# A values product of attention that is half native fp32 and half split operands

## The chip, the cores and the metric

The kernel runs on one core of a Trainium2 chip. The metric is the device time of one execution in microseconds (us): 1172.9 us before the change, the median of three runs that lie between 1172.45 and 1174.26 us.

## What is computed

The reference is a two-layer backbone over 512 latent tokens and 256 context tokens of width 1024. Layer 0 mixes tokens by pooling, layer 1 by attention, and each is followed by a squared-ReLU MLP with a hidden width of 4096. All inputs and the output are fp32. The change lies in the attention of layer 1, where 512 latent queries look at all 768 keys (6 tiles of 128), with 8 query heads of width 128 on 2 key/value heads:

```python
def attend(q, k, v):
    s = jnp.einsum('bqhgd,bkhd->bhgqk', q, k).astype(jnp.float32) * (HEAD_DIM ** -0.5)
    p = jax.nn.softmax(s, axis=-1).astype(v.dtype)
    return jnp.einsum('bhgqk,bkhd->bqhgd', p, v)
```

## The kernel before

**Split operands.** Almost every product is made of three TensorE matmuls: an fp32 operand is kept as a high half (`hi`, the value rounded to the reduced fp32 type `F32R`) and a low half (`lo`, the remainder), and hi·hi, hi·lo and lo·hi are added in PSUM. Each split costs one copy on ScalarE (ACT), which writes `hi`, and one subtraction on VectorE (DVE), which writes `lo`. A few products are native: both operands are plain fp32 and there is one matmul in the program.

**Order of the work.** The author places each helper at a time in a list (`Steps`), and the scheduler of the framework then sets the order on every engine from its own timing model. Each engine works its list in order, so an instruction that waits holds up all that stands behind it.

**Attention.** First the keys, values and queries are projected (`project`, L1064, tile `psq`); `kv_e` (L1120) splits the values of key tile t into `vH`, `vL` in the large buffer `rb`, and `kv_b`/`kv_c` normalise and transpose the keys. Then come 32 steps, `steps[i] = (h, t)`: head h (8) by block t of 128 queries (4). A step goes through these stages, each named by the line at which the profile shows it:

- `q_head` (once for a head): four transposes L1225 (tile `pq`), copy L1226 on ACT, subtraction L1227 on DVE.
- `s_scores`: six matmuls L1237 of 384 columns (tile `pss`, two PSUM tiles in turn), the row maximum L1241 on DVE, and the exponential L1242 on ACT, which also sums the row. It writes the row of 768 probabilities to one of four buffers, `pbuf(i % 4)`.
- `s_norm`: the reciprocal L1248 on DVE, and the scaling of the row, which a table of 32 truth values gives to DVE (L1250, 17 steps) or to ACT (L1252, 15 steps).
- `s_turn`: six transposes L1262 (tile `pspt`, one PSUM bank of the four of `psB` for each three key tiles), and for each three a copy L1264 on ACT and a subtraction L1265 on DVE, into `pTH` and `pTL`.
- `s_values` (after every second step, for 256 queries): 18 matmuls L1276 (tile `po`), three for each of the 6 key tiles, then copy L1278 on ACT and subtraction L1279 on DVE into `oH`, `oL`.

Between them stand the splits of the weights `w_o`, which follow attention: four loads of 1 MB into the three `raw` buffers, each split in quarters (L142 on ACT, L145 on DVE). Two of them are split during attention and two at its end, when `unit[1]` and `unit[2]` are free. These two units are one tile, `units`, opened once at the end of the first stage; during attention they hold `pTH`, `pTL` and the queries of the later heads. After attention comes the product with `w_o` (L1302, tile `psy`).

Of the kernel before, what the change touches and what calls it, by code (L numbers as in the profile page):

```python
# [17 lines left out]
P = 128  # L18
# [24 lines left out]
class Steps:  # L43
# [3 lines left out]
    def at(self, t, fn, *args):  # L47
        self.items.append((t, len(self.items), fn, args))
# [20 lines left out]
def backbone(ctx: ExitStack, tc, x, ctx_in, w_ada, w_pool, pool_scale, w_qkv, g_q, g_k, w_o, w_mlp_in,  # L69
# [39 lines left out]
    unit, pinned = [rb[:, 6144:10240]], [True]  # L109

    def open_units():
        rawe.close()
        pools[0] = rawp
        units = ctx.enter_context(tc.tile_pool(name="units", bufs=1)).tile([P, 2 * 4096], F32R, name="units")
        unit.extend(units[:, 4096 * i: 4096 * (i + 1)] for i in range(2))
# [35 lines left out]
    class Ring:  # L151
# [1 line left out]
            self.slots, self.n, self.halves = slots, 0, halves  # L153

        def load(self, src, width, pin=False, wait=None):
            raw = raw_load(src, rawp)
# [639 lines left out]
    st.at(200, open_units)  # L796
    st.run()

    pso = {}
# [233 lines left out]
    vH = rb[:, 3072:4608].rearrange("p (t n) -> p t n", n=256)  # L1033
    vL = rb[:, 4608:6144].rearrange("p (t n) -> p t n", n=256)
# [156 lines left out]
    def before0():  # L1191
# [8 lines left out]
        for t in (4, 5, 0, 1, 2, 3):  # L1200
# [6 lines left out]
    qTs = [(z[:, 0:512], z[:, 512:1024]) for z in (unit[0][:, 0:1024], unit[0][:, 1024:2048],  # L1207
                                                    unit[1][:, 3072:4096], unit[2][:, 3072:4096])]
    qbuf = lambda h: qTs[h if h < 2 else 2 + h % 2]
    pTH = unit[2][:, 0:NT * LAT].rearrange("p (s n) -> p s n", n=LAT)  # L1210
    pTL = unit[1][:, 0:NT * LAT].rearrange("p (s n) -> p s n", n=LAT)
    pbuf = lambda i: (xr[:, 4, 0:TOK], xr[:, 5, 0:TOK], gate[:, 1, 0:TOK], acc[:, 4 * D:4 * D + TOK])[i]
    aring = Ring([ra[:, 8192:12288], unit[0], unit[1], unit[2]])

    def wo_unit(ch, kk, wait=None):
        return aring.load(w_o[ch, kk], 512, True, wait)
# [29 lines left out]
    def s_norm(i):  # L1246
        sm, p = smx[i], pbuf(i % 4)
        ve.reciprocal(sm[:, 2:3], sm[:, 1:2])  # L1248
        if (False,False,False,True,False,True,True,True,True,True,True,True,False,False,True,False,True,False,True,False,True,True,True,False,False,True,False,False,False,False,True,True)[i]:
            ve.tensor_scalar(out=p, in0=p, scalar1=sm[:, 2:3], scalar2=None, op0=ALU.mult)  # L1250
        else:
            sc.activation(p, p, AF.Copy, scale=sm[:, 2:3])  # L1252

    def s_turn(i):
        _, t = steps[i]
        sl = slice(t * P, (t + 1) * P)
        p = pbuf(i % 4)
        for b in range(2):
            ps = psB.tile([P, 3, P], F32, tag="b", name="pspt")
            for j in range(3):  # L1260
                k = 3 * b + j
                te.transpose(ps[:, j, :], p[:, k * P:(k + 1) * P], ident)  # L1262
            hi, lo = pTH[:, 3 * b:3 * b + 3, sl], pTL[:, 3 * b:3 * b + 3, sl]
            sc.copy(hi, ps)  # L1264
            ve.tensor_tensor(out=lo, in0=ps, in1=hi, op=ALU.subtract)  # L1265

    def s_values(i):
        h, t = steps[i]
        half = t // 2
        kv = h // 4  # L1270
        hs = slice(kv * HD, (kv + 1) * HD)
        qs = slice(256 * half, 256 * half + 256)
        po = psB.tile([P, 512], F32, tag="b", name="po")
        for kt in range(NT):
            for n, (v, p) in enumerate(((vH, pTH), (vL, pTH), (vH, pTL))):
                te.matmul(po[:, 0:256], v[:, kt, hs], p[:, kt, qs],  # L1276
                          start=(kt == 0 and n == 0), stop=(kt == NT - 1 and n == 2))
        sc.copy(oH[:, h, qs], po[:, 0:256])  # L1278
        ve.tensor_tensor(out=oL[:, h, qs], in0=po[:, 0:256], in1=oH[:, h, qs], op=ALU.subtract)  # L1279

# [36 lines left out]
    def attention(st, base, unit_t):  # L1317
        at = lambda i, fn, *args: st.at(base + unit_t * i, fn, *args)
        for i, (h, t) in enumerate(steps):
            if t == 0:  # L1320
                at([-2, 3, 4.542, 7.928, 13.236, 15.602, 19.752, 23.755][h], q_head, h)
            at(i + 0.2, s_scores, i)
            at(i + 1.3, s_norm, i)
            at(i + 3.1, s_turn, i)
            if t % 2:
                at(i + 5.2, s_values, i)
        raws = []
# [134 lines left out]
```

## Time and profile before

| | us |
|---|---|
| median of three runs | 1172.9 |
| the profiled execution, its whole time | 1173.48 |
| its span in the trace | 1171.7 |
| TensorE (PE) busy | 1143.0 (98%) |
| weight loads (PEld) busy | 989.2 (84%) |
| VectorE (DVE) busy | 938.4 (80%) |
| ScalarE (ACT) busy | 636.7 (54%) |
| start of the first score matmul, of the last values matmul | 673.7, 780.0 |

Times in the trace count from the start of the span. A matmul's row shows the time from its issue to the end of its drain; matmuls that follow each other overlap, so the pace of a run of n equal ones is (time of the run − time of one) / (n − 1). A number in square brackets at the end of a row is idle time of the engine ahead of it and what ended it.

### The profile page before, as it was taken

The page shows a single profiled execution, that of the slowest core. Times are in us where ns is not written, and L with a number is a line of the kernel's source. Part 1 is how long each engine was busy: PE and PEld are TensorE (multiplying, and loading weights), DVE is VectorE, ACT ScalarE, POOL GpSimd, SP SyncE. Part 2 cuts the span into 40 slices and gives each one's busy share as a digit, 9 for nine tenths or more (in the row PEclk, how much of TensorE's full clock was granted, in tenths as well). Part 3 has the DMA queues.
Part 4 walks back from the last instruction along what each step waited for, and adds up shares of the span by engine and source line. Part 5 has one row for each costly group of instructions (what it writes and reads, how often), then busy time and mean ns, then how long its engine had stood idle before and what let it go on. Part 6 is the DMA issues. An engine that isn't in the chain of part 4 may idle for free.

```text
span 1171.7 us, 15966 instructions
## 1 busy us (share of the span) xinstructions
PE 1143.0 (98%) x6172; PEld 989.2 (84%) x6172; DVE 938.4 (80%) x1538; ACT 636.7 (54%) x1082; POOL 67.0 (6%) x120
## 2 busy tenths in 40 slices
PE   7899999999999999999999999999899999999997
PEld 5579899889899988998887889988888888888886
DVE  4688687989988997996778599877787779778876
ACT  4577655555454534555675388852776436535522
POOL 2030000000000000000241200001100000000001
PEclk9899999999999999999999999999999999999999
DMA  9884213343334334343423101115234124314312
GB/s 375 354 318 154 72 45 135 133 159 109 144 144 144 144 137 147 112 144 108 180 73 107 37 1 37 37 73 197 91 138 150 61 84 144 108 36 144 108 37 107
DMA packets 25516, 147.32 MB, mean 126 GB/s; under 512 B 2785, under 2 KB 5217, under 8 KB 9698
## 3 DMA queue, kind: packets, MB, share of 16 engines
q1 hardware_dynamic: 25442, 146.32, 34.2%
q8 instruction: 48, 0.79, 0.3%
q14 instruction: 26, 0.21, 0.1%
HBM read 138.96 MB, written 7.34 MB: 125 GB/s over the span
## 4 chain that ended last, share of the span: by engine, by line
PE 49%; issue 42%; POOL 3%; DVE 2%; ACT 2%; DMA 1%; SPq 0%; POOLq 0%; DVEq 0%; ACTq 0%
PE pso L817 22%; PE psin L691 18%; PE psin L567 3%; PE psq L1064 2%; PE pspool L65 1%; POOL rs L185 1%; PE psada L65 1%; PE pspool L490 1%; POOL rs L1073 1%; DMA raw<-in_w_ada 1%; DMA xr<-in_x 1%; PE psada L227 1%; POOL ms L183 1%; DVE ra L65 0%; ACT junk L170 0%
## 5 line engine op out<-in xcount | busy, mean ns | idle before, releaser
L817 PE MATMUL pso<-units,rb 128*128 128x512 f32 x1152 | 278.2, 392 | 0.0
L817 PEld LDWEIGHTS pso<-units,rb 128*128 128x128 f32 x1152 | 214.8, 188 | 41.2
L273 DVE SCALAR_TENSOR_TENSOR rows<-raw,cond,rows 128x256 f32<-128x256 f32 x280 | 126.5, 475 | 2.0
L829 DVE TENSOR_TENSOR acc<-acc,pso 128x512 f32<-128x512 f32 x129 | 85.1, 674 | 41.4 <-PE pso L817 41.2
L567 PE MATMUL psin<-ra,rb 128*128 128x512 f32 (+1 forms) x432 | 103.3, 340 | 1.8 <-ACT ra L364 1.6
L921 PE MATMUL pso<-units,pairs 128*128 128x512 f32 x336 | 82.3, 389 | 0.0
L567 PE MATMUL psin<-ra 128*128 128x512 f32 x256 | 80.5, 390 | 0.0
L567 PEld LDWEIGHTS psin<-ra,rb 128*128 128x128 f32 x432 | 69.9, 189 | 11.3 <-ACT ra L364 1.9
L921 PEld LDWEIGHTS pso<-units,pairs 128*128 128x128 f32 x336 | 63.1, 188 | 13.1
L925 DVE TENSOR_TENSOR acc<-acc,pso 128x512 f32<-128x512 f32 x72 | 48.7, 681 | 28.8 <-PE pso L921 28.8
L183 POOL TENSOR_SCALAR ms<-ss 128x1 f32<-128x1 f32 x20 | 11.4, 572 | 998.3 <-ACT junk L170 946.1
L691 PE MATMUL psin<-ra,units 128*128 128x384 f32 x336 | 65.5, 337 | 0.4 <-ACT psin L703 0.4
L691 PE MATMUL psin<-sums,units 128*128 128x384 f32 x336 | 63.9, 337 | 0.0
L691 PEld LDWEIGHTS psin<-ra,units 128*128 128x128 f32 x336 | 59.7, 188 | 3.9 <-ACT psin L703 0.9
L691 PEld LDWEIGHTS psin<-sums,units 128*128 128x128 f32 x336 | 58.9, 188 | 1.7
L145 DVE TENSOR_TENSOR units<-raw,units 128x1024 fp32r<-128x1024 f32 (+2 forms) x49 | 55.1, 1148 | 4.5 <-ACT units L142 4.4
L567 PEld LDWEIGHTS psin<-ra 128*128 128x128 f32 x256 | 48.0, 188 | 10.0
L142 ACT CAST units<-raw 128x1024 fp32r<-128x1024 f32 (+2 forms) x49 | 46.8, 994 | 14.0 <-PE pso L817 10.2
L827 ACT COPY acc<-pso 128x512 f32<-128x512 f32 x48 | 27.2, 588 | 48.9 <-PE pso L817 48.6
L567 PE MATMUL psin<-rb 128*128 128x512 f32 (+1 forms) x144 | 52.6, 367 | 0.2 <-DVE rb L365 0.2
L1064 PE MATMUL psq<-units,ra 128*128 128x512 f32 x216 | 51.7, 392 | 0.0
L567 PE MATMUL psin<-rb,ra 128*128 128x512 f32 x128 | 49.8, 389 | 0.0
(279 smaller groups left out, 2346.7 us busy)
## 6 DMA issues: line engine op xcount, KB each, us to landing
raw<-in_w_ada SPq DMA_DIRECT2D x48, 1024.0 KB, 4.9
raw<-in_w_mlp_in SPq DMA_DIRECT2D x32, 1024.0 KB, 4.9
raw<-in_w_mlp_out SPq DMA_DIRECT2D x32, 1024.0 KB, 5.3
raw<-in_w_qkv SPq DMA_DIRECT2D x6, 1024.0 KB, 4.8
spill<-xr SPq DMA_DIRECT2D x10, 512.0 KB, 4.2
xr<-spill SPq DMA_DIRECT2D x10, 512.0 KB, 6.8
raw<-in_w_o SPq DMA_DIRECT2D x4, 1024.0 KB, 4.8
xr<-in_x SPq DMA_DIRECT2D x4, 512.0 KB, 5.2
```

The costliest lines, as they stand in the source:

```text
L65: return lambda *args, **kw: self.tc.keep_in_program_order(f(*args, **kw))
L142: a = sc.copy(hi, raw)
L145: b = ve.tensor_tensor(out=lo, in0=raw, in1=hi, op=ALU.subtract)
L273: ve.scalar_tensor_tensor(out=r, in0=raw[:, k, :], scalar=cond[:, k, c:c + 1], in1=r, op0=ALU.mult, op1=ALU.add)
L567: te.matmul(ps[:, bank, o:o + ln], w[:, k, fs], rhs, start=start, stop=(k == KT - 1 and n == 2), skip_group_check=len(ks) < KT)
L691: te.matmul(bank, w[k], a[k], start=start and k == 0 and m == 0, stop=stop and k == 3 and m == 2, skip_group_check=True)
L817: te.matmul(pss[h][:, 0:cols[h][1]], a[:, f, ts_], w[:, f, cols[h][0]:sum(cols[h])], start=(n == 0 and not seeded[t]), stop=(n == len(seq) ...
L827: sc.copy(d, ps)
L829: ve.tensor_tensor(out=d, in0=d, in1=ps[:, 0:w], op=ALU.add)
L921: te.matmul(ps, a, w, start=(m == 0), stop=(m == len(seq) - 1))
L925: ve.tensor_tensor(out=M[n][:, t], in0=M[n][:, t], in1=ps, op=ALU.add)
L1064: te.matmul(ps, a[:, k, sl], w[:, k % 4, :], start=(k == 0 and n == 0), stop=(k == KT - 1 and n == 2))
```

## The change

**Values product.** Key tiles 0 to 2 are multiplied in native fp32 (one matmul in place of three), tiles 3 to 5 in split operands as before: 3 + 9 matmuls in place of 18. So the values of tiles 0 to 2 are copied as fp32 into `xr` row 4 and have no `lo`, and the first three transposed tiles of a step are copied as fp32 into `pT` and have no subtraction.

**Scaling.** All 32 rows are scaled on DVE; the table is gone.

**Buffers.** Two probability buffers, `pT`, the two halves `pTh` and the queries of heads 2 to 7 (`qs`) lie in a pool `soft`, which is opened over the memory of `units` at step 1.1 and closed at step 37.5, when `units` is opened anew. The last two `w_o` loads are issued at the same places as before, but get their unit only then. Normalised keys move to `xr` row 5 and have two buffers in place of four. The first stage is unchanged (`end_loads`).

The core of the diff:

```diff
+    values = lambda: xr[:, 4, 0:768].rearrange("p (t n) -> p t n", n=256)
+    vH = rb[:, 3072:3840].rearrange("p (t n) -> p t n", n=256)
+    vL = rb[:, 3840:4608].rearrange("p (t n) -> p t n", n=256)
...
     def kv_e(t):
         ps = pj[t]
-        sc.copy(vH[:, t, :], ps[:, 256:512])
-        ve.tensor_tensor(out=vL[:, t, :], in0=ps[:, 256:512], in1=vH[:, t, :], op=ALU.subtract)
+        if t < 3:
+            sc.copy(values()[:, t, :], ps[:, 256:512])
+        else:
+            sc.copy(vH[:, t - 3, :], ps[:, 256:512])
+            ve.tensor_tensor(out=vL[:, t - 3, :], in0=ps[:, 256:512], in1=vH[:, t - 3, :], op=ALU.subtract)
...
-        kf = xr[:, 4, 256 * (t % 4):256 * (t % 4) + 256]
+        kf = xr[:, 5, 512 + 256 * (t % 2):768 + 256 * (t % 2)]
...
+    def open_soft():
+        uheld[0].close()
+        pool = uheld[0].enter_context(tc.tile_pool(name="soft", bufs=1))
+        qs = pool.tile([P, 2 * 1024], F32R, name="qs")
+        qTs.extend((qs[:, 1024 * i:1024 * i + 512], qs[:, 1024 * i + 512:1024 * i + 1024]) for i in range(2))
+        halves = pool.tile([P, 2, 3, LAT], F32R, name="pTh")
+        soft["t"] = pool.tile([P, 3, LAT], F32, name="pT"), halves[:, 0], halves[:, 1]
+        ps = [pool.tile([P, TOK], F32, name=f"p{i}") for i in range(2)]
+        soft["p"] = ps
+
+    def close_soft():
+        uheld[0].close()
+        open_units()
+        aring.slots[2:] = unit[1:]
...
-        if (False,False,False,True,False,True,True,True,True,True,True,True,False,False,True,False,True,False,True,False,True,True,True,False,False,True,False,False,False,False,True,True)[i]:
-            ve.tensor_scalar(out=p, in0=p, scalar1=sm[:, 2:3], scalar2=None, op0=ALU.mult)
-        else:
-            sc.activation(p, p, AF.Copy, scale=sm[:, 2:3])
+        ve.tensor_scalar(out=p, in0=p, scalar1=sm[:, 2:3], scalar2=None, op0=ALU.mult)
...
-            hi, lo = pTH[:, 3 * b:3 * b + 3, sl], pTL[:, 3 * b:3 * b + 3, sl]
-            sc.copy(hi, ps)
-            ve.tensor_tensor(out=lo, in0=ps, in1=hi, op=ALU.subtract)
+            full, hi, lo = (z[:, :, sl] for z in soft["t"])
+            if b == 0:
+                sc.copy(full, ps)
+            else:
+                sc.copy(hi, ps)
+                ve.tensor_tensor(out=lo, in0=ps, in1=hi, op=ALU.subtract)
...
-        for kt in range(NT):
-            for n, (v, p) in enumerate(((vH, pTH), (vL, pTH), (vH, pTL))):
-                te.matmul(po[:, 0:256], v[:, kt, hs], p[:, kt, qs],
-                          start=(kt == 0 and n == 0), stop=(kt == NT - 1 and n == 2))
+        full, hi, lo = soft["t"]
+        seq = [(values()[:, kt, hs], full[:, kt, qs]) for kt in range(3)]
+        seq += [(v[:, kt, hs], p[:, kt, qs]) for kt in range(3) for v, p in ((vH, hi), (vL, hi), (vH, lo))]
+        for n, (v, p) in enumerate(seq):
+            te.matmul(po[:, 0:256], v, p, start=(n == 0), stop=(n == len(seq) - 1))
...
+        at(1.1, open_soft)
+        at(37.5, close_soft)
...
         for kk in range(2):
-            at((23.386, 25.741)[kk], lambda kk: wo[1].append(wo_unit(1, kk, raws)), kk)
+            at((23.386, 25.741)[kk], lambda kk: late.append(raw_load(w_o[1, kk], rawp)), kk)
+            at(37.6, lambda kk: wo[1].append(aring.place(late[kk], 512, raws)), kk)
```

**What moves.** The scheduler orders anew what stands in attention. On TensorE, from the sixth values product on, the order was (scores `pss`, transposes `pspt`, values `po`):

```order
L1276 MATMUL po<-units,rb 128x256 x18
L1262 MATMUL pspt<-ident,gate 128x128 x3
L1237 MATMUL pss<-rb,units 128x384 x6
L1262 MATMUL pspt<-ident,gate 128x128 x3
L1262 MATMUL pspt<-ident,acc 128x128 x6
L1276 MATMUL po<-units,rb 128x256 x18
L1237 MATMUL pss<-rb,units 128x384 x6
```

and in the changed kernel, whose scores stand at L1261, transposes at L1283 and values at L1302 (`p_5952` and `p_5953` are the two new probability buffers):

```order
L1302 MATMUL po<-pT,xr 128x256 x3
L1302 MATMUL po<-pTh,rb 128x256 x9
L1261 MATMUL pss<-rb,qs 128x384 x6
L1283 MATMUL pspt<-ident,p_5953 128x128 x6
L1261 MATMUL pss<-rb,qs 128x384 x5
L1283 MATMUL pspt<-ident,acc 128x128 x3
L1261 MATMUL pss<-rb,qs 128x384
```

The scores and transposes keep their places between the values products; the product itself becomes three native matmuls and nine on halves.

On DVE, around the second quarter of the first `w_o` split (L145), the order before was (L1241 maximum, L1250 scaling, L1265 subtraction of a transposed half, L1279 subtraction of an output half):

```order
L145 TENSOR_TENSOR ra<-raw,ra 128x512
L1279 TENSOR_TENSOR ra<-po,ra 128x256
L1248 RECIPROCAL sm<-sm 128x1
L1241 TENSOR_REDUCE sm<-pss 128x1
L1250 TENSOR_SCALAR gate<-gate,sm 128x768
L1265 TENSOR_TENSOR units<-pspt,units 128x3x128 x2
L1250 TENSOR_SCALAR acc<-acc,sm 128x768
L1241 TENSOR_REDUCE sm<-pss 128x1
```

and around the same quarter now (there L143; maximum L1265, reciprocal L1272, scaling L1273, subtractions L1289 and L1304):

```order
L143 TENSOR_TENSOR ra<-raw,ra 128x512
L1304 TENSOR_TENSOR ra<-po,ra 128x256
L1265 TENSOR_REDUCE sm<-pss 128x1
L1289 TENSOR_TENSOR pTh<-pspt,pTh 128x3x128
L1265 TENSOR_REDUCE sm<-pss 128x1
L1272 RECIPROCAL sm<-sm 128x1
L1273 TENSOR_SCALAR acc<-acc,sm 128x768
L1289 TENSOR_TENSOR pTh<-pspt,pTh 128x3x128
L1272 RECIPROCAL sm<-sm 128x1
L1273 TENSOR_SCALAR gate<-gate,sm 128x768
```

Each step now has one subtraction where it had two, and one scaling in every step.

On ACT, at the end of attention (L1264 copies of transposed rows, L1278 copies of outputs, L142 the eight quarters of the last two `w_o` units), the order was:

```order
L1278 CAST ra<-po 128x256
L1264 CAST units<-pspt 128x3x128 x4
L1278 CAST ra<-po 128x256
L142 CAST units<-raw 128x512 x8
L1278 CAST ra<-po 128x256
L305 COPY gate<-psg 128x512 x2
```

and is now (L1286 and L1288 the copies of transposed rows, L1303 those of outputs, L140 the quarters):

```order
L1286 COPY pT<-pspt 128x3x128
L1288 CAST pTh<-pspt 128x3x128
L1303 CAST ra<-po 128x256 x2
L140 CAST units<-raw 128x512 x8
L305 COPY gate<-psg 128x512 x2
```

The quarters have moved behind the copy of the last output. Outside of attention TensorE's order is the same but for a few rows.

More of the change, by code (lines that the diff above doesn't have):

```diff
@@ L108, in backbone @@
     pools = [rawe.enter_context(tc.tile_pool(name="rawe", bufs=4))]
-    unit, pinned = [rb[:, 6144:10240]], [True]
+    unit, pinned, uheld = [rb[:, 6144:10240]], [True], [ctx.enter_context(ExitStack())]
     def open_units():
[L112 to L115, printed above, removed]
+        units = uheld[0].enter_context(tc.tile_pool(name="units", bufs=1)).tile([P, 2 * 4096], F32R, name="units")
+        unit[1:] = [units[:, 4096 * i: 4096 * (i + 1)] for i in range(2)]
     minus = phase[:, 0:2 * KT].rearrange("p (k c) -> p k c", c=2)
@@ L155, in load, with place @@
         def load(self, src, width, pin=False, wait=None):
-            raw = raw_load(src, rawp)
+            return self.place(raw_load(src, rawp), width, wait, pin)
+        def place(self, raw, width, wait=None, pin=False):
             s = self.slots[self.n % len(self.slots)]
@@ L795, in backbone, with end_loads @@
             st.at(max(z + 2.4, 63.4 + q / 10) if q < 3 else 76.5 + 2 * f + t / 10, parts0, t, q, f)
-    st.at(200, open_units)
+    def end_loads():
+        rawe.close()
+        pools[0] = rawp
+        open_units()
+    st.at(200, end_loads)
     st.run()
@@ L1032, in backbone @@
     kTL = rb[:, 1536:3072].rearrange("p (h n) -> p h n", n=TOK)
-    vH = rb[:, 3072:4608].rearrange("p (t n) -> p t n", n=256)
-    vL = rb[:, 4608:6144].rearrange("p (t n) -> p t n", n=256)
     q32 = acc[:, 0:NL * D].rearrange("p (t n) -> p t n", n=D)
@@ L1206, in backbone @@
     oL = ra[:, 4096:8192].rearrange("p (h n) -> p h n", n=LAT)
-    qTs = [(z[:, 0:512], z[:, 512:1024]) for z in (unit[0][:, 0:1024], unit[0][:, 1024:2048],
-                                                    unit[1][:, 3072:4096], unit[2][:, 3072:4096])]
+    qTs = [(z[:, 0:512], z[:, 512:1024]) for z in (unit[0][:, 0:1024], unit[0][:, 1024:2048])]
     qbuf = lambda h: qTs[h if h < 2 else 2 + h % 2]
[L1210 to L1213, printed above, removed]
+    aring = Ring([ra[:, 8192:12288], unit[0], None, None])
+    soft = {}
+    def open_soft():
[9 more added lines that the diff above has]
+        uheld[0].close()
+        open_units()
+        aring.slots[2:] = unit[1:]
+    pbuf = lambda i: soft["p"][i - 1] if i in (1, 2) else (gate[:, 1, 0:TOK], acc[:, 4 * D:4 * D + TOK])[i // 2]
     def wo_unit(ch, kk, wait=None):
@@ L1326, in attention @@
                 at(i + 5.2, s_values, i)
-        raws = []
+        raws, late = [], []
+        at(1.1, open_soft)
+        at(37.5, close_soft)
         at(7, lambda: wo[0].append(wo_unit(0, 0, raws)))
```

## The prediction

> **What bounds the kernel now.** I read the profile page's busy shares first, then busy time by stretches of attention, then TensorE's timeline there.
>
> ```profile
> PE 1143.0 (98%) x6172; PEld 989.2 (84%) x6172; DVE 938.4 (80%) x1538; ACT 636.7 (54%) x1082; POOL 67.0 (6%) x120
> ```
> ```profile
> 672.00:693.00 21.00, 19.23 (x107) 16.46 (x106) 18.56 (x36) 14.92 (x39) 2.85 (x5) 1.00 0.00 0
> ...
> 700.00:710.00 10.00, 10.00 (x77) 9.89 (x77) 10.00 (x23) 7.74 (x18) 0.00 (x0) 1.00 0.00 0
> 710.00:720.00 10.00, 8.47 (x63) 7.92 (x63) 9.85 (x20) 8.86 (x20) 0.00 (x0) 1.00 0.11 16
> 720.00:730.00 10.00, 9.82 (x72) 9.30 (x72) 8.50 (x18) 7.17 (x17) 0.00 (x0) 1.00 0.22 92
> 730.00:740.00 10.00, 9.57 (x72) 9.20 (x71) 9.62 (x20) 9.11 (x21) 0.00 (x0) 1.00 0.01 2
> ...
> 770.00:782.00 12.00, 11.48 (x93) 10.60 (x92) 7.70 (x16) 7.67 (x19) 0.00 (x0) 1.00 0.01 2
> ```
>
> Columns of the second fence: stretch, its length, busy PE, PEld, DVE, ACT, POOL, then the clock. TensorE bounds the program (98%), but in attention DVE is as full: 10.00 and 9.85 of 10 us from 700 to 720. TensorE waits a little there, and idle time as printed leaves out the 0.27 us in which the last matmul drains. So I reckon by pace:
>
> ```profile
> L1276 PE MATMUL po<-units,rb x288: 277/283/386, 693.0 to 780.0; 128*128 128x256 f32 x144
> ```
> ```profile
> 695.26 1.21 PE L1237 MATMUL pss<-rb 128*128 128x384 f32 x6
> 696.31 0.82 PE L1262 MATMUL pspt<-ident,xr 128*128 128x128 f32 x6
> ```
> ```profile
> 693.02 2.40 PE L1276 MATMUL po<-units,rb 128*128 128x256 f32 x18
> ...
> 711.92 2.39 PE L1276 MATMUL po<-units,rb 128*128 128x256 f32 x18 [0.41 <-DVE units L1265]
> 719.27 2.38 PE L1276 MATMUL po<-units,rb 128*128 128x256 f32 x18 [1.11 <-DVE sm L1248]
> 727.02 2.31 PE L1276 MATMUL po<-units,rb 128*128 128x256 f32 x18
> ```
> ```profile
> 769.47 1.63 PE L1262 MATMUL pspt<-ident,xr 128*128 128x128 f32 x12
> 771.55 2.41 PE L1276 MATMUL po<-units,rb 128*128 128x256 f32 x18 [0.44 <-DVE units L1265]
> ...
> 781.60 0.71 PE L1302 MATMUL psy<-ra 128*128 128x512 f32 x2
> ```
>
> A values matmul takes (2.31 − 0.28)/17 = 0.119 us, a score matmul (1.21 − 0.34)/5 = 0.174, a transpose (0.82 − 0.27)/5 = 0.110. From the first values product (693.02) to the first matmul after attention (781.60) lie 288 values, 150 scores (25 steps), 168 transposes (28 steps), 20 query transposes and 16 gate matmuls at 0.11: 34.3 + 26.1 + 18.5 + 2.2 + 1.8 = 82.9 of 88.6 us. So **5.7 us** are lost to waits. The largest: 719.27 (1.3), 771.55 (769.47 + 12 × 0.110 = 770.79, so 0.8) and 711.92 (0.6).
>
> What ends them is DVE's queue:
>
> ```profile
> 709.84 0.94 DVE L1241 TENSOR_REDUCE sm<-pss 128x1 f32<-128x768 f32 x1
> 710.70 0.61 DVE L1250 TENSOR_SCALAR gate<-gate,sm 128x768 f32<-128x768 f32 x1
> 711.23 1.01 DVE L1265 TENSOR_TENSOR units<-pspt,units 128x384 fp32r<-128x384 f32 x2
> ...
> 717.10 0.96 DVE L1241 TENSOR_REDUCE sm<-pss 128x1 f32<-128x768 f32 x1
> 717.98 0.68 DVE L145 TENSOR_TENSOR ra<-raw,ra 128x512 fp32r<-128x512 f32 x1
> 718.58 0.55 DVE L1265 TENSOR_TENSOR units<-pspt,units 128x384 fp32r<-128x384 f32 x1
> ```
>
> The subtraction that releases the product at 719.27 starts only at 718.58, behind a maximum and a quarter of a `w_o` split; it ends at 719.13. It is the subtractions that the change halves.
>
> **Term 1: native products, on TensorE's path.** The nearest native matmuls are those of the first stage:
>
> ```profile
> 17.73 1.09 PE L65 MATMUL psc<-gate,acc 128*128 128x136 f32 x8
> ```
> ```profile
> L303 PE MATMUL psg<-ident,gc x16: 270/275/275, 779.1 to 781.6; 128*128 128x128 f32 x16
> ```
> ```profile
> L227 PE MATMUL psada<-raw,cond x80: 379/379/617, 64.4 to 85.0; 128*32 128x256 f32 x64, 128*32 128x512 f32 x16
> ```
> ```profile
> L65 PE MATMUL psada<-raw,cond x144: 376/592/659, 19.0 to 57.6; 128*32 128x512 f32 x80, 128*32 128x256 f32 x64
> ```
>
> L303 writes eight products and shows sixteen rows: a native product is two records. A record of 136 columns takes (1.09 − 0.28)/7 = 0.116 us; 256 more columns take 0.592 − 0.379 = 0.213. So a record of 256 columns takes 0.116 + 0.120 × 0.213/0.256 = 0.216, a native product 0.432, and three of them 1.295 us where nine values matmuls took 9 × 0.119 = 1.07. That is +0.22 us for each of 16 values products: **+3.5 us**. Bounds: by columns alone 0.213 a record, +3.2; by the 136-column record scaled up whole, 0.218, +3.8. The first change of kind, native to halves, exists already (transposes to values); I cost it at nothing, since the run at 693.02 takes 2.40 in place of 2.31 and the last transpose before it is that much shorter.
>
> A rule that speaks against the change: the Trainium skill, "FP8 and Floating Point Precision", section TensorE Precision Notes, has true fp32 as four passes, and "TensorE: Matmul & The Clock Gate", section Back-to-back issue gap, has N/2.4 + 2.5 ns a matmul. By these a key tile costs 0.437 native against 0.328 in halves, an estimated +5.2 us in all. The four passes agree with the trace (two records at two cycles a column); the gap does not, since a matmul on halves takes 0.119, not 0.109.
>
> **Term 2: waits that go.**
>
> ```profile
> L1265 DVE TENSOR_TENSOR units<-pspt,units 128x384 fp32r<-128x384 f32 x64 | 33.5, 547 | 0.3 <-ACT units L1264 0.2
> ...
> L1252 ACT ACTIVATE xr<-xr,sm 128x768 f32<-128x768 f32 x9 | 8.5, 948 | 0.2 <-DVE sm L1248 0.2
> L1279 DVE TENSOR_TENSOR ra<-po,ra 128x256 fp32r<-128x256 f32 x15 | 6.3, 417 | 5.8 <-ACT ra L1278 5.8
> ```
>
> Back to back a DVE instruction takes 0.08 less than its row (710.70 to 711.23: 0.53). DVE loses 32 subtractions at 0.47 (−15.0) and gains 15 scalings at 0.53 (+8.0); ACT loses 15 scalings at 0.86 (−13). For two steps with one values product, DVE then needs two maxima 1.72, two reciprocals 0.14, two subtractions 0.94, two scalings 1.06, an output subtraction 0.34, half a query subtraction 0.3 and a `w_o` quarter 0.6: 5.1 us. Before, where both scalings lay on DVE, it needed 6.0. TensorE needed 2.09 + 1.32 + 2.14 + 0.22 = 5.8 and will need 6.0. So DVE was the slower of the two in that stretch and will have 0.9 us to spare; ACT has more. In the new order two steps' transposes stand between a subtraction and the product that reads it. I let 4.2 of the 5.7 us go and 1.5 stay: small unevenness 0.8, and 0.7 from instructions queued badly. Bounds: nothing goes (0), everything but the unevenness goes (4.9).
>
> **Term 3: the first steps.**
>
> ```profile
> 685.26 1.33 PE L1237 MATMUL pss<-rb 128*128 128x384 f32 x6 [0.44 <-ACT gate L1242]
> ...
> 689.52 1.32 PE L1237 MATMUL pss<-rb 128*128 128x384 f32 x6 [0.94 <-ACT acc L1242]
> ```
>
> About 3 us are lost here before 693.02, since scores wait for an exponential to free one of two PSUM tiles. Steps 0, 1, 2 and 4 are scaled on ACT now and will be on DVE, in front of the maximum of step 3. Behind it wait the exponential and then the scores. I followed the new order through with these durations: step 1's scaling +0.53, one subtraction fewer −0.47, and the fourth step's transposes come 0.1 to 0.2 us later: **+0.2** (bounds −2.5, +1).
>
> **Small terms.** During projection TensorE waits for a DVE subtraction:
>
> ```profile
> 623.40 2.56 PE L1064 MATMUL psq<-rb,ra 128*128 128x512 f32 x10 [0.65 <-DVE ra L370]
> ```
>
> The new order puts two key transposes into that wait: −0.2. The late `w_o` quarters cost nothing: ACT starts them after the last output copy, some 3.5 us later than here,
>
> ```profile
> 778.22 4.26 ACT L142 CAST units<-raw 128x512 fp32r<-128x512 f32 x8
> ```
> ```profile
> 792.60 5.60 PE L1302 MATMUL psy<-units,ra 128*128 128x512 f32 x24
> ```
>
> and their first reader starts 11 us after attention ends; eight DVE quarters at 0.6 fit in. They hold two `raw` buffers 2 to 3 us longer, so the next loads on SP's queue move by as much; without the 5 us that are left, that delay would reach the path. The two key buffers are free in time: each key's transposes stand ahead of the second key after it.
>
> **Sum.** +3.5 − 4.2 + 0.2 − 0.2 = −0.7 us. The profiled execution took 1173.48 us, so 1172.8; the median lies 0.6 below it, so **1172.2 us**. 0.2% is 2.3 us, about what a measurement of this kernel can tell from no change.
>
> **Rivals.**
> - *Waits stay, the native price is paid (slower).* If TensorE's waits come from the order and the two PSUM score tiles, not from DVE's load, less than 1.2 of the 5.7 us goes, and the sum passes +2.3; with none gone it is +3.5, 1176.4 us. For: the waits at 685.26 and 689.52 are of this kind. Against: DVE's 10.00 of 10 us at 700 to 710, and the row at 718.58.
> - *The start gains too (faster).* ACT's four early scalings are gone, so the exponentials come earlier and 2.5 of the 3 us before 693 go: −0.7 − 2.7 = −3.4, 1169.5. Against: DVE, which gets the scalings, still normalises the last queries there (18.56 of 21 us).
> - *A dearer native record.* If the 0.012 us by which a values matmul exceeds its columns (0.119 against 0.107) belongs to its weight load, the 96 native records pay it too: +1.0, 1173.2. By the gap of the Trainium skill's "TensorE: Matmul & The Clock Gate", section Back-to-back issue gap, an estimate gives 1173.9. Against: the 136-column records, whose weights are as wide, exceed theirs by 0.003.
>
> **Chances.** Forecast 0.55, waits stay 0.20, start gains 0.15, dearer record 0.10. The forecast's own range is 1170.6 to 1174. The range 1170.0 to 1175.6 leaves out most of the second rival and the upper half of the first. Faster by over 0.2%: the second rival and a little of the forecast, 0.18; slower: most of the first, 0.20; within 0.2%: 0.62.
>
> **What would show it.** Native values records at 0.216 us pace; nine halves still at 0.119; the stretch from first values product to the first matmul after attention at 87.9 us where it was 88.6; DVE below 9 of 10 us from 700 to 720; no wait of over 0.5 us ahead of a values product. I would be wrong if TensorE still waits for DVE or ACT by 4 us or more in that stretch, or if the stretch before it shrinks by over 1 us.

## The result and the profile after

| | before | forecast | after |
|---|---|---|---|
| median, us | 1173.68 (20 runs) | 1172.2 (beside 1172.9) | 1170.87 (20 runs, 1169.02 to 1175.43) |
| ratio to before, 95% interval | | 0.9994 | 0.9981 [0.9975, 0.9988] |

The change makes the kernel some 2 us faster: the interval lies wholly below 1, and the ratio is just under the 0.2% at which the prediction drew its line. Applied to the 1172.9 us of the prediction it gives 1170.7, at the lower edge of the forecast's own range (1170.6 to 1174). A second measurement of the same kernel beside other runs of the kernel before gave 0.9978 [0.9969, 0.9987]. The sign was right. The terms behind it are larger than forecast on both sides, and they nearly cancel.

**Which part of the trace may be compared.** The first profile of the changed kernel (span 1173.6) is longer than that of before (1171.7), although its median is shorter. The reason lies ahead of the change and behind attention (see the last section), so below I compare stretches between fixed points of the program: *projection* (first to last `psq` matmul), *start* (last `psq` matmul to first values product), *values* (first values product to the first matmul after attention, `psy`). "Lost" is a stretch less TensorE's need in it, counted by the paces of the prediction (native record 0.216 us). A second profile of the changed kernel gives each stretch again within 0.05 us.

| us | before | after | forecast of the difference |
|---|---|---|---|
| projection | 82.10 | 81.93 | −0.2 |
| start (lost) | 13.05 (3.0) | 13.41 (3.4) | +0.2 |
| values, TensorE's need | 82.8 | 86.4 | +3.5 |
| values, lost | 5.8 | 0.3 | −4.2 |
| values, whole | 88.58 | 86.71 | −0.7 |

The first of these fences is the busy line of the changed kernel's page, the second its busy time in the stretches that the prediction showed, and the whole values stretch.

```profile
PE 1147.6 (98%) x6124; PEld 993.3 (85%) x6124; DVE 934.4 (80%) x1518; ACT 625.9 (53%) x1067; POOL 68.6 (6%) x120
```
```profile
700.00:710.00 10.00, 10.00 (x69) 9.58 (x68) 9.20 (x19) 8.15 (x19) 0.00 (x0) 1.00 0.00 0
710.00:720.00 10.00, 10.00 (x71) 9.63 (x70) 8.99 (x17) 7.14 (x17) 0.00 (x0) 1.00 0.01 2
720.00:730.00 10.00, 10.00 (x70) 9.64 (x69) 9.82 (x21) 7.64 (x19) 0.00 (x0) 1.00 0.27 105
730.00:740.00 10.00, 10.00 (x70) 9.56 (x69) 8.71 (x17) 8.22 (x20) 0.00 (x0) 1.00 0.01 2
...
695.51:782.22 86.71, 86.71 (x597) 83.04 (x595) 72.06 (x140) 61.85 (x141) 0.00 (x0) 1.00 0.07 26
```

TensorE (first number after the length) has no idle time left in the values stretch: 86.71 of 86.71. (A wait that is shorter than the drain of the matmul ahead of it does not show in the busy time, so "lost" goes by pace.) The page's 98% says the same before and after. Before, the whole stretch read so (TensorE 85.55 of 88.58, DVE 77.21):

```profile
693.02:781.60 88.58, 85.55 (x645) 82.39 (x644) 77.21 (x159) 72.89 (x159) 0.00 (x0) 1.00 0.07 25
```

In TensorE's timeline of the changed kernel a product now is two rows, six native records and nine matmuls on halves, and none has a wait in brackets:

```profile
718.91 0.82 PE L1283 MATMUL pspt<-ident,acc 128*128 128x128 f32 x6
719.56 1.46 PE L1302 MATMUL po<-pT,xr 128*128 128x256 f32 x6
720.67 1.42 PE L1302 MATMUL po<-pTh,rb 128*128 128x256 f32 x9
721.93 1.21 PE L1261 MATMUL pss<-rb,qs 128*128 128x384 f32 x6
```

From the one's start to the next work it takes 721.93 − 719.56 = 2.37 us, and 6 × 0.216 + 9 × 0.119 is 2.37. Before, 18 matmuls by pace took 2.14. So a product costs 0.225 us more, sixteen of them 3.6 us.

### The profile page after: what moved, and what is told of

Same layout as the page of the kernel before. It is cut to its first block, busy times and chain, and to the rows that moved or that the text cites. A ratio compares the mean times of both kernels' runs of the same rounds, so it can differ in the third digit from the quotient of the medians.

```text
span 1173.6 us, 15880 instructions
## 1 busy us (share of the span) xinstructions
PE 1147.6 (98%) x6124; PEld 993.3 (85%) x6124; DVE 934.4 (80%) x1518; ACT 625.9 (53%) x1067; POOL 68.6 (6%) x120
## 4 chain that ended last, share of the span: by engine, by line
PE 49%; issue 42%; POOL 3%; DVE 3%; DMA 2%; ACT 1%; SPq 0%; POOLq 0%; DVEq 0%; ACTq 0%
PE pso L822 22%; PE psin L691 18%; PE psin L567 3%; PE psq L1067 2%; DMA raw<-in_w_ada 1%; PE pspool L65 1%; POOL rs L185 1%; PE psada L65 1%; PE pspool L490 1%; POOL rs L1076 1%; DMA xr<-in_x 1%; PE psada L227 1%; DVE ra L65 0%; POOL ms L183 0%; ACT junk L170 0%
## 5 line engine op out<-in xcount | busy, mean ns | idle before, releaser
L143 DVE TENSOR_TENSOR units<-raw,units 128x1024 fp32r<-128x1024 f32 (+2 forms) x49 | 55.1, 1149 | 3.9 <-ACT units L140 3.7
L140 ACT CAST units<-raw 128x1024 fp32r<-128x1024 f32 (+2 forms) x49 | 46.8, 995 | 14.3 <-PE pso L822 10.2
```

The lines of the kernel that those rows point to most:

```text
L140: a = sc.copy(hi, raw)
L143: b = ve.tensor_tensor(out=lo, in0=raw, in1=hi, op=ALU.subtract)
```

## The experiments

All stretches are from one profile of each kernel, all ratios are to runs of the kernel before on the same chip. The trace decides where a time went. The ratio confirms it only to about 1 us.

| kernel | start (lost) | values (lost) | start + values | ratio [95%] |
|---|---|---|---|---|
| before | 13.05 (3.0) | 88.58 (5.8) | 101.63 | |
| after, second time (a_again) | 13.42 (3.4) | 86.71 (0.3) | 100.12 | 0.9978 [0.9969, 0.9987] |
| a_table | 12.01 (2.0) | 86.82 (0.4) | 98.83 | 0.9970 [0.9959, 0.9980] |
| a_dummy_sub | 16.92 (4.8) | 90.14 (5.8) | 107.06 | 1.0039 [1.0026, 1.0051] |
| b_no_lo | 12.01 (2.0) | 83.41 (0.6) | 95.42 | 0.9951 [0.9939, 0.9964] |
| a_early_act | 12.03 (2.0) | 86.63 (0.2) | 98.65 | 0.9979 [0.9970, 0.9988] |
| b_all_dve | 16.95 (4.9) | 88.54 (7.8) | 105.49 | 1.0037 [1.0024, 1.0051] |
| b_later2 | 13.02 (3.0) | 90.31 (7.5) | 103.33 | 1.0016 [1.0004, 1.0028] |
| b_even | 13.01 (3.0) | 86.81 (4.0) | 99.82 | 0.9970 [0.9958, 0.9982] |
| a_one_native | 12.64 (2.6) | 85.31 (1.3) | 97.95 | 0.9971 [0.9960, 0.9981] |
| a_best | 12.15 (2.1) | 85.34 (0.1) | 97.49 | 0.9955 [0.9942, 0.9967] |
| a_best_again | 12.15 (2.1) | 85.35 (0.1) | 97.50 | 0.9965 [0.9952, 0.9978] |

Each edit also lets the scheduler order attention anew; this can't be held fixed. In a_dummy_sub and b_all_dve it put one step's scores (2.09 us) ahead of the first values product, so for them read the sum of both stretches and the losses.

**The changed kernel again (a_again).** No edit.

> The changed kernel itself once more, as the measure for the others and to see how far two profiles of one program differ. From the last projection matmul to the first matmul after attention its first profile shows 100.1 us (13.4 before the first values product, 86.7 behind it), where the kernel before has 101.6 (13.05 and 88.6). Every theory expects 100.1 within 0.2 and 2 to 2.5 us less than the kernel before. If the first profile was odd, the stretches come out over 0.5 us from these.

It held: 13.42 and 86.71. Medians 1170.66 against 1173.70 us.

**The old table of scalings on the changed kernel (a_table).**

```diff
-        ve.tensor_scalar(out=p, in0=p, scalar1=sm[:, 2:3], scalar2=None, op0=ALU.mult)
+        if (False,False,False,True,False,True,True,True,True,True,True,True,False,False,True,False,True,False,True,False,True,True,True,False,False,True,False,False,False,False,True,True)[i]:
+            ve.tensor_scalar(out=p, in0=p, scalar1=sm[:, 2:3], scalar2=None, op0=ALU.mult)
+        else:
+            sc.activation(p, p, AF.Copy, scale=sm[:, 2:3])
```

> The changed kernel with the old table of scalings: 15 of 32 rows are scaled on ACT again. Theory of the forecast (DVE's load made the waits and the subtractions are what relieved it): DVE gets 8 us lighter still, so from the first values product to the first matmul after attention the stretch stays at 86.4 to 87.2 us; the start, whose four early scalings go back to ACT, shrinks from 13.4 to about 13.1. Time as the changed kernel's within 0.6 us. Rival (freeing ACT of its 15 scalings of 0.86 us is what took the waits away): the stretch goes back to 88 us or more, the time up by 1.5 to 3 us.

```profile
692.70:779.52 86.82, 86.82 (x596) 83.16 (x595) 65.53 (x129) 70.49 (x154) 0.00 (x0) 1.00 0.07 25
```

ACT is nearly as full as before the change again (70.49, the last but one engine, where it was 72.89) and nothing comes back: freeing ACT took no wait away. The scaling's move to DVE thus brought nothing in the values stretch. At the start it costs 1.4 us, where I had expected 0.3.

**The removed subtractions done again for nothing (a_dummy_sub).**

```diff
             if b == 0:
                 sc.copy(full, ps)
+                ve.tensor_tensor(out=xr[:, 5, 0:384].rearrange("p (j n) -> p j n", n=P), in0=ps, in1=full, op=ALU.subtract)
```

> The changed kernel with the 32 subtractions of the first three tiles done again on DVE, their result written to free space that nothing reads: DVE's load as if the halves had stayed, while no product waits for these subtractions. Theory of the forecast (load): DVE needs about 6.0 us for two steps, as TensorE does, and the waits come back: 88.5 to 91 us behind the first values product in place of 86.7, 2 to 4 us more time than the changed kernel. Rival (the product waited because those subtractions were the last link ahead of it, not because DVE was full): nothing waits for them now, 86.5 to 87.2 us and the time of the changed kernel within 0.6.

The losses are those of the kernel before again, and more: 5.8 us behind the first values product, 4.8 at the start; 6.9 us over both stretches, where I had expected 2 to 4. No product reads what these subtractions write. But they take time on DVE, and they also hold the PSUM bank of the three transposes until they have read it: three products, at 712.15, 774.12 and 778.29, are released by the dummy itself, which costs 0.6 us together by pace. This is how a wait for DVE's queue looks, on TensorE and then on DVE:

```profile
717.82 0.82 PE L1283 MATMUL pspt<-ident,acc 128*128 128x128 f32 x6
719.31 1.56 PE L1303 MATMUL po<-pT,xr 128*128 128x256 f32 x6 [0.67 <-DVE pTh L1290]
```
```profile
717.37 0.55 DVE L1287 TENSOR_TENSOR xr<-pspt,pT 128x384 f32<-128x384 f32 x1
717.84 0.95 DVE L1265 TENSOR_REDUCE sm<-pss 128x1 f32<-128x768 f32 x1
718.71 0.55 DVE L1290 TENSOR_TENSOR pTh<-pspt,pTh 128x384 fp32r<-128x384 f32 x1
```

L1287 is the dummy. The subtraction that the product needs (L1290) starts behind it and a maximum, as in the kernel before. More of the loss, 3.2 of the 5.8 us, lies ahead of five scores that wait for an exponential, and each time the exponential stands on ACT behind a copy that had waited for transposes. The longest of them, on ACT and then on TensorE:

```profile
743.84 0.48 ACT L1286 COPY pT<-pspt 128x384 f32<-128x384 f32 x1 [1.06 <-PE pspt L1283]
744.22 0.49 ACT L1289 CAST pTh<-pspt 128x384 fp32r<-128x384 f32 x1
744.59 0.92 ACT L1266 ACTIVATE p<-pss,sm 128x768 f32<-128x768 f32 x1
```
```profile
745.65 0.62 PE L1261 MATMUL pss<-rb,qs 128*128 128x384 f32 x2 [0.92 <-ACT p L1266]
```

Here it is not DVE's queue that TensorE waits for but the order that the scheduler made for the fuller DVE. So this run shows that the subtractions bring the waits; it does not separate DVE's queue, the PSUM banks and the new order from each other.

**The kernel before without half of the subtractions (b_no_lo).**

```diff
             sc.copy(hi, ps)
-            ve.tensor_tensor(out=lo, in0=ps, in1=hi, op=ALU.subtract)
+            if b:
+                ve.tensor_tensor(out=lo, in0=ps, in1=hi, op=ALU.subtract)
...
-            for n, (v, p) in enumerate(((vH, pTH), (vL, pTH), (vH, pTL))):
+            for n, (v, p) in enumerate(((vH, pTH), (vL, pTH), (vH, pTL if kt >= 3 else pTH))):
```

> The kernel before without the subtraction of key tiles 0 to 2 in every step; the third product of these tiles reads the high half again, so the low half of the probabilities of three tiles is left out of the result. TensorE has the same matmuls (82.9 us by pace behind the first values product), DVE 15 us less. Theory of the forecast (the 5.7 us of waits are DVE's subtractions): 83.5 to 85 us in that stretch, 3.5 to 5 us less time than the kernel before. Rival (the waits are those of the order and of two PSUM score tiles): 87.5 us or more, at most 1 us less time.

```profile
690.94:774.35 83.41, 83.41 (x644) 82.28 (x643) 66.93 (x131) 71.89 (x158) 0.00 (x0) 1.00 0.08 27
```

The third product of three tiles adds the high halves a second time here, so the result is not the reference's; the work of TensorE is the same. DVE is at 66.9 in place of 77.2 us, ACT nearly as before (71.9, it was 72.9), and 5.2 of the 5.8 us are gone; 1.0 more at the start. Between this run and the last, the rival "waits stay" is excluded: without these subtractions nearly all of the waits go, and with them done again as much comes back. How much of it runs through DVE's queue and how much through the order that the scheduler makes for it stays open, since both edits changed the order too.

**Early rows on ACT (a_early_act).**

```diff
-        ve.tensor_scalar(out=p, in0=p, scalar1=sm[:, 2:3], scalar2=None, op0=ALU.mult)
+        if i in (0, 1, 2, 4):
+            sc.activation(p, p, AF.Copy, scale=sm[:, 2:3])
+        else:
+            ve.tensor_scalar(out=p, in0=p, scalar1=sm[:, 2:3], scalar2=None, op0=ALU.mult)
```

> The changed kernel with the rows of steps 0, 1, 2 and 4 scaled on ACT, all others on DVE. If the 1.4 us that the old table gained at the start (13.41 to 12.01 us from the last projection matmul to the first values product) come from these four scalings, which stand in DVE's queue behind the last queries' normalisation, the start is 12.0 again, the stretch behind it 86.7, together 98.8, and the time 1.2 us below the changed kernel's. Rival (they come from the order that the whole table gives): 13 us or more at the start.

The start is 12.03: the four early scalings alone are what a_table gained. The changed kernel's start on DVE, ACT and TensorE, one fence each:

```profile
687.50 0.62 DVE L1273 TENSOR_SCALAR p<-p,sm 128x768 f32<-128x768 f32 x1
688.03 0.95 DVE L1265 TENSOR_REDUCE sm<-pss 128x1 f32<-128x768 f32 x1
```
```profile
689.08 0.48 ACT L1286 COPY pT<-pspt 128x384 f32<-128x384 f32 x1 [1.39 <-PE pspt L1283]
689.45 0.48 ACT L1288 CAST pTh<-pspt 128x384 fp32r<-128x384 f32 x1
689.84 0.59 ACT L1250 CAST qs<-pq 128x512 fp32r<-128x512 f32 x1
690.32 0.91 ACT L1266 ACTIVATE acc<-pss,sm 128x768 f32<-128x768 f32 x1
```
```profile
688.55 0.82 PE L1283 MATMUL pspt<-ident,p 128*128 128x128 f32 x6
...
691.37 1.34 PE L1261 MATMUL pss<-rb 128*128 128x384 f32 x6 [1.57 <-ACT acc L1266]
```

And with the early rows on ACT (this profile runs 4.75 us earlier, by the last `psq` matmuls at 677.35 and 682.10), DVE, ACT and TensorE again:

```profile
682.75 0.95 DVE L1265 TENSOR_REDUCE sm<-pss 128x1 f32<-128x768 f32 x1
```
```profile
682.81 1.93 ACT L1274 ACTIVATE p<-p,sm 128x768 f32<-128x768 f32 x2
684.65 0.88 ACT L1266 ACTIVATE acc<-pss,sm 128x768 f32<-128x768 f32 x1
685.43 0.19 ACT L1266 ACTIVATION_READ_ACCUMULATOR acc<-pss,sm 128x1 f32 x1
685.53 0.46 ACT L1289 COPY pT<-pspt 128x384 f32<-128x384 f32 x1
```
```profile
683.84 0.88 PE L1286 MATMUL pspt<-ident,p 128*128 128x128 f32 x6
...
685.67 1.31 PE L1261 MATMUL pss<-rb 128*128 128x384 f32 x6 [0.18 <-ACT acc L1266]
```

The maximum of step 3 starts at 687.50 on the other's clock in place of 688.03: the 0.53 us of the scaling ahead of it. But that isn't what the exponential waits for. It comes at 689.40 in place of 690.32, and in the changed kernel the maximum had ended at 688.98: there the exponential stands behind three copies on ACT, the first of which waits 1.39 us for transposes. These start at the same time in both (688.55, and 683.84 + 4.75 = 688.59), behind scores on TensorE. With the early rows on ACT, its two scalings (682.81) fill the time of that wait and the exponential stands ahead of the copies. So the scores that need the PSUM tile wait 1.57 us there and 0.18 here, and start 0.95 us earlier. The whole time, 0.9979, doesn't tell this gain from the changed kernel's runs; the trace does.

**All rows on DVE in the kernel before (b_all_dve).** The table is replaced by the one line that a_table takes out.

> The kernel before with only one part of the change: all 32 rows scaled on DVE. DVE gets 8 us more, some 6.0 us for every two steps, TensorE's need stays at 82.9 us behind the first values product and 5.8 for two steps. Load theory: waits grow from 5.8 to 8 or more, 91 us or more there, 2 us or more slower than the kernel before. Rival (the waits don't come from DVE's load): 88.6 within 0.7.

Lost: 7.8 in the values stretch, and 4.9 at the start in place of 3.0, so 3.9 us more over both. The absolute length that I had named (91) was wrong because a step's scores moved ahead of the stretch; the loss is close to what the load theory had (8 or more). As in a_dummy_sub, most of it, 5.4 of the 7.8 us by pace, lies ahead of scores that wait for ACT.

**Products placed later (b_later, b_later2).**

```diff
-                at(i + 5.2, s_values, i)
+                at(i + 6.0, s_values, i)
```

> The kernel before with each values product placed one step later in the list; no work is added or taken away. The scheduler then lays the products in pieces between scores and transposes. If the waits were those of the order (a product that stands too close behind the subtractions it reads), at most 1.5 of the 5.8 us stay: 84.3 us or less behind the first values product. If DVE's load sets them, which is the same as before, 3.5 us or more stay: 86.3 or more.

With 6.2 (b_later) the products came to stand behind the transposes that write their columns anew, read a later step's columns and waited for them: 107.71 us for start and values, ratio 1.0056 [1.0043, 1.0070]. It tells nothing of the order. With 6.0:

> The kernel before with each values product placed 0.8 of a step later in the list, ahead of the transposes that write its columns anew; the work is the same. (The run with a whole step put it behind them, so its products read columns of a later step and waited for those: it says nothing on the order.) If the waits were those of the order, at most 1.5 of the 5.8 us stay: 84.3 us or less behind the first values product. If DVE's load sets them, 3.5 us or more stay: 86.3 or more.

7.5 us are lost, more than before, with the same DVE time (77.6). This other order of the same work does not take the waits away; it adds 1.7 us. That no order would, one run cannot show.

**The trade-off from the other side (a_best, a_one_native).** Two native tiles, or one, in place of three. a_best differs from a_early_act in sizes and in where two buffers lie:

```diff
-    values = lambda: xr[:, 4, 0:768].rearrange("p (t n) -> p t n", n=256)
+    values = lambda: xr[:, 4, 0:512].rearrange("p (t n) -> p t n", n=256)
...
-            for j in range(3):
-                k = 3 * b + j
+            for j in range(2 + 2 * b):
+                k = 2 * b + j
...
-        seq = [(values()[:, kt, hs], full[:, kt, qs]) for kt in range(3)]
-        seq += [(v[:, kt, hs], p[:, kt, qs]) for kt in range(3) for v, p in ((vH, hi), (vL, hi), (vH, lo))]
+        seq = [(values()[:, kt, hs], full[:, kt, qs]) for kt in range(2)]
+        seq += [(v[:, kt, hs], p[:, kt, qs]) for kt in range(4) for v, p in ((vH, hi), (vL, hi), (vH, lo))]
```

> Two native key tiles and four in halves, with the rows of steps 0, 1, 2 and 4 scaled on ACT. TensorE saves 0.073 us for each of 16 products, 1.17 us (85.2 by pace behind the first values product in place of 86.4); DVE subtracts four tiles of a step in place of three, about 0.13 us more for a step, some 5.4 us for two steps where TensorE has 5.9. If the native price is linear and DVE has room for this: 85.3 to 85.9 us behind the first values product, 12.0 to 12.5 at the start, about 2.4 us below the changed kernel. Rival (the fourth tile's subtraction brings the waits back): over 86.7 us there, no faster than the changed kernel with the early scalings on ACT.

> One native key tile and five in halves, rows of steps 0, 1, 2 and 4 scaled on ACT. TensorE's need behind the first values product is 1.17 us less than with two native tiles, 84.0. DVE subtracts five tiles a step, in two instructions, some 0.2 us a step more: about 5.8 us for two steps where TensorE has 5.85. Load theory: with no room left on DVE waits of 1.5 us or more come back, 85.5 us or more, no gain over two native tiles (85.3). Rival (DVE's load is not what decides): 84.2 to 84.6 us, 1 us below two native tiles.

> Two native tiles with the early scalings on ACT once more, beside the kernel with one native tile on one chip: 97.5 us from the last projection matmul to the first matmul after attention, 0.45% below the kernel before. If the first time was a lucky draw, it is 0.3% or less.

The rows of the whole values stretch, two native tiles and then one:

```profile
691.02:776.36 85.34, 85.34 (x611) 82.78 (x611) 73.88 (x139) 61.53 (x142) 0.00 (x0) 1.00 0.08 26
```
```profile
690.22:775.53 85.31, 85.31 (x628) 82.29 (x627) 78.21 (x168) 64.15 (x171) 0.00 (x0) 1.00 0.07 26
```

From three native tiles to two the stretch falls by 86.63 − 85.34 = 1.29 us, of which the native price is 1.20 (86.41 − 85.21 by pace) and no wait comes back. From two to one TensorE's need falls by 1.2 again and 1.2 us of waits come back (1.3 lost): nothing gained. Both rows read as wholly busy, since these waits are short: pieces of 0.1 to 0.2 us at native products and transposes, and those of which the trace names the end, end with a subtraction on DVE. Two native tiles with the early rows on ACT is the best kernel of this study: 97.5 us in attention where the changed kernel has 100.1, medians 1168.0 and 1168.5, ratio 0.9955 and 0.9965. The second ratio lies between the two expectations (0.45% and 0.3%); the stretches repeat (97.49 and 97.50).

**The old work with an even table (b_even).** a_one_native lost 1.3 us with DVE at 78.2 of 84.0 us of TensorE's need, the kernel before 5.8 with 77.2 of 82.8. So DVE's mean share isn't all.

```diff
-        if (False,False,False,True,False,True,True,True,True,True,True,True,False,False,True,False,True,False,True,False,True,True,True,False,False,True,False,False,False,False,True,True)[i]:
+        if i not in (0, 1, 2, 4, 6, 8, 10, 12, 14, 16, 18, 22, 24, 28, 30):
```

> The kernel before with another table of scalings: 17 on DVE and 15 on ACT as before, steps 0, 1, 2 and 4 on ACT as before, but from step 6 on one row of each pair of steps on each engine, apart from the pairs 20/21 and 26/27, which lie on DVE alone. No subtraction is dropped and no product is native; TensorE's need stays 82.8 us behind the first values product and DVE's busy time about 77. One native tile lost only 1.3 us there with DVE busy for as large a part of TensorE's need (78.2 of 84.0) as in the kernel before (77.2 of 82.8, 5.8 us lost). If the unevenness of the old table (three pairs in a row wholly on DVE) made the difference: 2 us or less lost, 84.8 or less in the stretch, 1.5 us or more below the changed kernel's. If it lies in the chains of the order, not in how the scalings lie: 4 us or more lost, 86.8 or more.

```profile
692.93:779.75 86.82, 85.20 (x646) 82.23 (x644) 77.31 (x159) 72.52 (x159) 0.00 (x0) 1.00 0.08 26
```

With the same DVE time, 4.0 us are lost in place of 5.8: just within the second expectation. The uneven table, with the order that it brought, accounts for some 1.8 us. A table of truth values alone, with no native product, gives 99.82 us, no worse than the changed kernel's 100.12. Why the old work still loses 4.0 where one native tile loses 1.3 stays open but for the largest piece. Transposes wait there for a PSUM bank; the subtraction that frees it (L1279) needs the copy of an output (L1278), which stands on ACT behind a scaling. On ACT and on TensorE:

```profile
767.53 0.93 ACT L1252 ACTIVATE gate<-gate,sm 128x768 f32<-128x768 f32 x1
768.36 0.36 ACT L1278 CAST ra<-po 128x256 fp32r<-128x256 f32 x1
```
```profile
769.23 0.55 PE L1262 MATMUL pspt<-ident,xr 128*128 128x128 f32 x3 [0.90 <-DVE ra L1279]
```

By pace this is 1.1 of the 4.0 us, and here ACT's queue holds TensorE up. In a_one_native all scalings but the four early ones lie on DVE, ACT is busy for 64.2 us in place of 72.5, and only five of six tiles need a subtraction.

## Why the prediction was right, point by point

- **Term 1, the native price (+3.5): right.** Measured +3.6, by 2.37 against 2.14 us for a product; one native tile less (a_best against a_early_act) shortens the stretch by 1.29 us, where a third of 3.6 is 1.20. The rival of a dearer record falls: the record takes (1.46 − 0.38)/5 = 0.216, whatever its weight load. By the Trainium skill, "TensorE: Matmul & The Clock Gate", section Back-to-back issue gap, a matmul at the full clock comes N/2.4 + 2.5 ns after the one before it; with two cycles a column a record of 256 comes to an estimated 215.8 ns, and the trace agrees (0.216 us). For halves, where the formula gives an estimated 109 ns, the trace keeps 119. So the estimate of +5.2 that I made from this page failed on the halves, not on the native record.
- **Term 2, the waits that go (−4.2, bounds 0 to −4.9): right in cause, too small in size.** Measured −5.5, outside my bounds. The step that failed is "I let 4.2 of the 5.7 us go and 1.5 stay: small unevenness 0.8, and 0.7 from instructions queued badly": 0.3 stayed. The unevenness, which I took as a floor, mostly goes too when DVE has room (b_no_lo: 0.6 left, a_best: 0.1). That the subtractions are the cause is shown by taking them away (b_no_lo) and by adding them again (a_dummy_sub). The path was only in part the one that I had named, DVE's queue ahead of a values product: by pace four waits for a subtraction make 2.7 of the 5.8 us before, and 1.4 lie ahead of three scores that wait for an exponential. My forecast of DVE under 9 of 10 us from 700 to 720 missed in the first ten (9.20) and held in the second (8.99).
- **The scaling's move, which I had netted into Term 2**: it takes no wait away (a_table) and by itself adds 2.0 us there (b_all_dve). In the values stretch it is harmless only since the subtractions are gone.
- **Term 3, the start (+0.2): right in sum, partly by luck, from two larger parts.** The subtractions that are dropped give −1.0 (b_no_lo), the four early scalings' move to DVE costs +1.4 (a_early_act); measured +0.4. I had followed DVE's queue but not ACT's, where the exponential came to stand behind copies that wait for transposes.
- **Small terms.** Projection −0.2: measured −0.17 and, in the second profile, −0.12; the wait of 0.65 us that I named is 0.35 in the first profile (625.86). The late `w_o` quarters: counted from the last projection matmul ACT starts them at 99.1 us (781.21 − 682.10) where it was 98.2 (778.22 − 679.98), so 0.9 later and not 3.5, and their reader does not wait:

```profile
781.21 4.27 ACT L140 CAST units<-raw 128x512 fp32r<-128x512 f32 x8
```
```profile
790.50 2.88 PE L1327 MATMUL psy<-rb,ra 128*128 128x512 f32 x12
793.22 5.60 PE L1327 MATMUL psy<-units,ra 128*128 128x512 f32 x24
```

- **The rivals.** "Waits stay" is excluded above. "The start gains too" did not happen, and with the early rows left on ACT it would have been 1.0 us, not 2.5.

Summed by the trace: −0.17 + 0.37 + 3.6 − 5.5 = −1.7 us, where I had −0.7; the medians say −2.8 with a ratio whose interval, on 1173.7 us, is −1.4 to −2.9 us. Of the 1 us by which the trace's sum passes mine, Term 2 makes 1.3, and the other terms give 0.3 back. By my own bounds for Term 2 the sum could have come out anywhere from +3.5 to −1.4 us, so the sign rested on the size that I had chosen within them, and that size was too small.

## What to carry to other kernels

Where an engine beside the bottleneck is as full as the bottleneck itself, count work for each repeated unit on both: a trade that costs the bottleneck 3.6 us paid because it took an estimated 15 us of subtractions (32 at 0.47) from the neighbour, and the best point was where the neighbour just had room (DVE at 0.87 of TensorE's need; at 0.93 waits came back). Take one load off at a time: here two thirds of the native tiles and none of the early scalings gave more than the whole change, and a more even table without any native product gave as much. When a helper is moved to another queue, follow both queues at the first steps, since what stands ahead of the next exponential there is on the path.

## What the hardware showed beside this

The program is the same in all these kernels up to the projection, yet the first projection matmul is issued anywhere from 595.3 to 600.3 us. It goes with the rate of the loads in the first 50 us: over the fourteen profiles the start comes the later the lower the rate, from 376 GB/s to 345. The rows of that window, with clock, DMA share and GB/s at the end, and the matmuls that follow, for the first profile of the changed kernel and for a_early_act, in turn:

```profile
0.00:50.00 50.00, 39.07 (x296) 26.84 (x296) 25.89 (x55) 23.65 (x38) 7.61 (x18) 0.90 0.87 345
```
```profile
L1067 PE MATMUL psq<-rb,ra x120: 389/389/504, 600.2 to 658.7; 128*128 128x512 f32 x120
```
```profile
0.00:50.00 50.00, 40.05 (x340) 26.68 (x340) 27.65 (x59) 26.59 (x46) 8.74 (x22) 1.00 0.93 376
```
```profile
L1067 PE MATMUL psq<-rb,ra x120: 389/389/501, 595.4 to 654.0; 128*128 128x512 f32 x120
```

The granted clock goes the same way (0.90 and 1.00), but it doesn't order the profiles, and the rate does. The kernel before has a lower clock than the second profile of the changed kernel and a higher rate, and its projection starts earlier (597.9 against 598.2):

```profile
0.00:50.00 50.00, 38.92 (x320) 26.91 (x324) 26.61 (x57) 24.61 (x41) 7.78 (x19) 0.93 0.89 354
```
```profile
0.00:50.00 50.00, 39.91 (x320) 28.10 (x324) 26.63 (x56) 24.34 (x41) 7.67 (x18) 0.97 0.90 352
```

So the loads seem to lead; no run was made that sets the two apart.

There is a second such place behind attention. From the first `psy` matmul to the end of the span ten profiles take 389.9 to 390.3 us, and four (the changed kernel's first, b_no_lo, b_later, b_even) 391.4 to 391.6. In these four the granted clock falls for some 3.4 us at one place, right behind two waits of TensorE of 1.6 us each that all have. The changed kernel's first and second profile there, 19 against 30 matmuls:

```profile
840.00:843.50 3.50, 3.50 (x19) 3.50 (x19) 2.64 (x4) 3.28 (x4) 0.00 (x0) 0.55 0.02 5
```
```profile
838.00:841.50 3.50, 3.50 (x30) 3.50 (x31) 2.63 (x4) 3.39 (x4) 0.00 (x0) 1.00 0.02 5
```

What decides whether the clock falls is not shown. Of the 3.4 us between the spans of these two profiles, 2.0 come from the start of the projection and 1.5 from here, while the stretches in between repeat within 0.05 us. It is why a gain of 1 to 3 us is better read from such a stretch than from a whole time.
